# Output projections of two branches as streams of their own beside attention, and weights loaded once per layer

## Chip, cores and metric

The kernel runs on one core of a Trainium2 chip. The metric is the device time of one execution in microseconds (us), the median of several runs.

## What is computed

One inference step of a backbone with two layers, over 1024 latent and 128 context tokens (T = 1152, nine blocks of 128), model width 1024. Cut to what the change touches:

```python
h = RMSNorm(x) * (1 + scale) + shift
P = h @ W_in                       # columns for three mixers A, B, C, their paths z, and merge logits G
o_A = diff_attention(...)          # 4 heads, two softmax maps each
o_B = retention, both directions   # 4 heads
o_C = gated DeltaNet, both directions   # 4 heads
y_b = (norm(o_b) * silu(z_b)) @ W_b              # W_b: 512 x 1024, for each of the three branches
x = x + gate * ((sum_b sigmoid(G_b) * y_b) @ W_out)   # W_out: 1024 x 1024
```

Branch 0 is A, 1 is B, 2 is C.

## The kernel before

Activations lie feature by token: `hH` and `hL` hold the 1024 features of all 1152 tokens as a high and a low part. A product of full precision is made from three matmuls, high x high, high x low and low x high. A weight block is therefore loaded (512 KB, DMA queue of SyncE), cast to its high part on ScalarE (L362) and subtracted to its low part on GpSimd (L363), all in `load_w`. Two shapes use it: `proj_feat` (L403: 24 matmuls of 384 tokens for a third of one block of 128 features) and `proj_tok` (L382: 24 matmuls of 256 features for 128 tokens). Working memory is 25 large buffers of 1160 values a partition (`pg`), 8 of 512 (`pm`) and a region of small ones (`lo`).

Each layer is a set of streams, written as generators: `rp0`, `rp1` (projections of retention heads 0, 1 and 2, 3, `ret_proj`), `rm0`, `rm1` (their chunks, `ret_mix`), `fk`, `fq`, `fv`, `mid`, `pp`, `scan` for each DeltaNet head, `av`, `prep`, `mix` for attention (`att_v`, `att_prep`, `att_mix`), twelve `z` and 24 `g` streams for paths and merge gates, `ada` for the modulation and `fin` for the final stage. The class `Emitter` issues one piece of a stream at a time. A chain stream (`CHAIN`) goes first when its latency has passed on an estimated clock, otherwise the first in the table `BULK` that may run; a stream starts when the streams that it names are done and `NEED` large buffers are free. What is issued is then ordered once more on each engine by the framework's scheduler, with leads given to some (`LEAD`, `EVAC`). Projections so stand between the steps of the chains on TensorE.

`scan` runs over the four DeltaNet heads, and `mix` behind it over the four attention heads. One step of `mix` is a block of 128 queries: two transposes of the query (L1447), 12 score matmuls against the keys (L1467), maxima on VectorE (L1468), exponentials on ScalarE (L1471), the weighted difference of the two maps on VectorE (L1478, once per step), nine transposes of it (L1489) and the products with the values (L1498). `rp1` waits for the last `prep` and `rm1` for the last `mix`.

Each head's output goes through `put_o` into DRAM (`osc`), each merge gate's tanh into `ssc`. The final stage (`finish`) takes three blocks of 384 tokens one after the other. For a block and each branch, in the order C, A, B, it loads the outputs and splits them (L1545, L1546), then goes through four weight blocks of `w_branch`: a unit is 12 matmuls of 384 columns (L1598), a gate load (L1592), and VectorE's product with the gate (L1601, L1603) and sum (L1604); the last branch's sums go into `hH` and `hL` (L1606, L1607). Then eight weight blocks of `w_out` are multiplied, 256 features at a time (L1637), gated and added to x (L1643, L1644), and normed for the next layer (`norm_rows`, `norm_cols`: L619, L632, L639). So all weights of the stage are loaded and split three times per layer: 36 blocks of `w_branch` and 24 of `w_out`.

Of the kernel before, what the change touches and what calls it, by code (L numbers as in the profile page):

```python
# [13 lines left out]
DEPTH = 2  # L14
NT = 9
NL = 8
# [25 lines left out]
BULK = "rp0 z20 g22 fk1 fk0 z10 fq2 g23 z11 fq1 g20 g21 fq0 fv0 g24 g00 fk3 fv1 gate0 g26 g25 g05 fv2 z21 fk2 g27 z22 prep0 z00 g03 z23 g01 fv3 g02 prep1 av0 fq3 g07 g04 g11 z13 z02 rp1 prep2 z03 g10 g06 z01 g14 g15 g12 g17 prep3 z12 av1 ada g16 g13 fin".split()  # L42
NEED = {'rp': 10, 'rm': 6, 'fk': 6, 'mid': 4, 'fq': 5, 'fv': 6, 'pp': 2, 'scan': 1, 'av': 10, 'prep': 9, 'mix': 5, 'z': 3, 'g': 3, 'gate': 5, 'ada': 6, 'fin': 10}
# [228 lines left out]
class Build:  # L272
# [3 lines left out]
    def run(self, upto=None):  # L276
        nc, tc = self.nc, self.tc
        with ExitStack() as ctx:
# [25 lines left out]
            self.zsc = [[[dr([128, T], f"zsc{i}_{b}_{h}") for h in range(NH)] for b in range(3)] for i in L]  # L304
            self.m1 = [[dr([72, 1024], f"m1_{i}_{h}") for h in range(NH)] for i in L]
# [129 lines left out]
    def layer(self, l):  # L435
# [17 lines left out]
        add("rm0", self.ret_mix(l, 0, r[0]), ("rp0",))  # L453

# [14 lines left out]
        add("rp1", self.ret_proj(l, 1, r[1]), ("prep3",))  # L469
        add("rm1", self.ret_mix(l, 1, r[1]), ("rp1", "mix3"))  # L470

# [10 lines left out]
        rest = [n(x) for x in gs + zs + ["rp1"] + ["ada"] * (not last)]  # L482
        add("fin", self.finish(l, rest), ["scan3", "mix3", "rp1", "g26", "g27"] + ["gate0"] * (l == 0))
# [301 lines left out]
    def ret_proj(self, l, p, s):  # L785
        nc, ar = self.nc, self.ar
        if p == 0:
            cs = self.load_cs()
# [17 lines left out]
        (cs if p == 0 else self.att["cs"]).free()  # L806
# [553 lines left out]
    def att_prep(self, l, h):  # L1360
# [63 lines left out]
        if h == NH - 1:  # L1424
            self.att["wq"].free()

# [104 lines left out]
    def finish(self, l, rest):  # L1531
        nc, ar, ap = self.nc, self.ar, self.ap
        last = l == DEPTH - 1
        gate = None
        orr = Ring(ar, 384, 3)
        BR = (2, 0, 1)

        def load_o(tb, br):
            blocks = [ar.alloc(PAGE, True) for _ in range(3)]
            hl = []  # L1540
            for h in range(NH):
                o = orr.next().v(384)
                nc.sync.dma_start(out=o, in_=self.osc[l][br][h][:, tb * 384:tb * 384 + 384])
                x = [blocks[i // 3].ap[:, (i % 3) * 384:(i % 3) * 384 + 384] for i in (2 * h, 2 * h + 1)]
                nc.scalar.copy(x[0], o)  # L1545
                nc.vector.tensor_tensor(out=x[1], in0=o, in1=x[0].bitcast(F32), op=ALU.subtract)  # L1546
                hl.append(x)
            return blocks, hl

        todo = [(tb, br) for tb in range(3) for br in BR]  # L1550
        names = {1: "rm1", 2: "scan3", 0: "mix3"}
        pend = []

        def ahead():
            if todo:
                tb, br = todo[0]
                if tb == 0:
                    yield (f"{names[br]}.{l}", f"g{br}6.{l}", f"g{br}7.{l}")
                    self.store(0)
                todo.pop(0)  # L1560
                pend.append(load_o(tb, br))

        seq = []
        for _ in range(3):
            seq += [ap["w_branch"][l, br, :, fp * 256:fp * 256 + 256] for br in BR for fp in range(4)]
            seq += [ap["w_out"][l, q * 512:(q + 1) * 512, n * 256:(n + 1) * 256] for n in range(4) for q in range(2)]
        held = []

        def weights():
# [3 lines left out]
            return held.pop(0)  # L1573

        yield from ahead()
        for tb in range(3):
            c = slice(tb * 384, tb * 384 + 384)
            acc = [ar.alloc(T) for _ in range(3)]
            yv = [acc[f // 3].v(3, 384)[:, f % 3] for f in range(8)]
# [130 lines left out]
```

## Time and profile before

| | |
|---|---|
| median of 3 runs | 3506.38 us (3504.82 to 3514.66) |
| profiled execution | 3519.01 us, span 3517.2 us, mean granted TensorE clock 0.955 |
| TensorE matmul / weight load busy | 92% / 88% |
| VectorE, ScalarE, GpSimd busy | 62%, 41%, 33% |
| DMA | 340 MB, mean 97 GB/s |

In the profile PE is TensorE's matmul, PEld its weight load, DVE VectorE, ACT ScalarE, POOL GpSimd and SP SyncE. Matmuls are pipelined, and the duration of one, some 0.3 us, is longer than the distance between the starts of two; so the price of a matmul is read from a dense run, its length over its count, and not from its mean. A line can be a helper's: L362 and L363 stand for all weight splits. The granted clock is 1.00 at 2.4 GHz and 0.50 at 1.2 GHz.

### The profile page before, as it was taken

The page shows a single profiled execution, that of the slowest core. Times are in us where ns is not written, and L with a number is a line of the kernel's source. Part 1 is how long each engine was busy: PE and PEld are TensorE (multiplying, and loading weights), DVE is VectorE, ACT ScalarE, POOL GpSimd, SP SyncE. Part 2 cuts the span into 40 slices and gives each one's busy share as a digit, 9 for nine tenths or more (in the row PEclk, how much of TensorE's full clock was granted, in tenths as well). Part 3 has the DMA queues.
Part 4 walks back from the last instruction along what each step waited for, and adds up shares of the span by engine and source line. Part 5 has one row for each costly group of instructions (what it writes and reads, how often), then busy time and mean ns, then how long its engine had stood idle before and what let it go on. Part 6 is the DMA issues. An engine that isn't in the chain of part 4 may idle for free. (4 is left out here: it accounts for less than half of the span.)

```text
span 3517.2 us, 61428 instructions
## 1 busy us (share of the span) xinstructions
PE 3231.1 (92%) x23275; PEld 3086.3 (88%) x23275; DVE 2171.8 (62%) x5053; ACT 1439.6 (41%) x4110; POOL 1144.2 (33%) x1134
## 2 busy tenths in 40 slices
PE   6999999999999987778899999999999998787899
PEld 5998899998998887668899998999999997786898
DVE  6555646645735775667675556665457376666776
ACT  4334444533434444433333354443434344443232
POOL 3122433244310430144551224332453133102454
PEclk7999999999999998889999999999999998899999
DMA  6134223232144011356541323222221210013665
GB/s 209 44 115 125 75 81 88 83 84 68 37 139 135 24 32 38 98 168 201 186 140 51 110 71 96 85 74 82 81 71 38 81 35 29 26 32 124 224 215 173
DMA packets 353723, 340.07 MB, mean 97 GB/s; under 512 B 57108, under 2 KB 325778, under 8 KB 353426
## 3 DMA queue, kind: packets, MB, share of 16 engines
q1 hardware_dynamic: 353426, 336.14, 30.4%
q8 instruction: 183, 3.00, 0.3%
q14 instruction: 114, 0.93, 0.1%
HBM read 262.50 MB, written 73.56 MB: 96 GB/s over the span
## 5 line engine op out<-in xcount | busy, mean ns | idle before, releaser
L403 PE MATMUL ps<-hH,pg 128*128 128x384 f32 x4608 | 1249.7, 345 | 11.8 <-ACT pg L667 4.7
L363 POOL TENSOR_TENSOR pg<-pg,pg 128x1024 fp32r<-128x1024 f32 x256 | 630.6, 2470 | 1117.0 <-ACT pg L362 675.8
L403 PEld LDWEIGHTS ps<-hH,pg 128*128 128x128 f32 x4608 | 838.7, 190 | 19.4 <-ACT pg L667 6.3
L403 PE MATMUL ps<-hL,pg 128*128 128x384 f32 x2304 | 792.3, 344 | 0.0
L382 PE MATMUL ps<-pg,hH 128*128 128x256 f32 (+1 forms) x2880 | 565.0, 291 | 22.1 <-POOL pg L363 5.4
L382 PEld LDWEIGHTS ps<-pg,hH 128*128 128x128 f32 x2880 | 462.0, 193 | 28.9 <-POOL pg L363 6.6
L403 PEld LDWEIGHTS ps<-hL,pg 128*128 128x128 f32 x2304 | 437.0, 190 | 1.2
L362 ACT CAST pg<-pg 128x1024 fp32r<-128x1024 f32 (+1 forms) x256 | 267.6, 1048 | 395.3 <-DMA pg<-in_w_in 144.9
L382 PE MATMUL ps<-pg,hL 128*128 128x256 f32 (+1 forms) x1440 | 414.1, 288 | 0.0
L1598 PE MATMUL ps<-pg,pg 128*128 128x384 f32 x1728 | 331.0, 352 | 44.0 <-ACT pg L362 19.2
L1598 PEld LDWEIGHTS ps<-pg,pg 128*128 128x128 f32 x1728 | 317.1, 198 | 51.9 <-ACT pg L362 21.5
L382 PEld LDWEIGHTS ps<-pg,hL 128*128 128x128 f32 x1440 | 277.5, 193 | 0.1
L341 POOL TENSOR_TENSOR lo<-lo,kc 128x3 f32<-128x3 f32 (+4 forms) x88 | 132.3, 1505 | 441.6 <-DVE lo L1524 125.4
L1467 PE MATMUL ps<-pg,pm 128*128 128x384 f32 x768 | 210.8, 377 | 43.3 <-ACT pg L1471 43.1
L1468 DVE TENSOR_REDUCE lo<-ps 128x1 f32<-128x384 f32 (+1 forms) x350 | 182.5, 540 | 100.4 <-PE ps L1467 97.5
L1471 ACT ACTIVATE pg<-ps,lo 128x384 f32<-128x384 f32 (+1 forms) x350 | 196.1, 570 | 101.5 <-DVE lo L1469 100.0
L1637 PE MATMUL ps<-pg,hH 128*128 128x256 f32 x1152 | 216.9, 291 | 11.9 <-ACT hH L1606 10.8
L1637 PEld LDWEIGHTS ps<-pg,hH 128*128 128x128 f32 x1152 | 186.4, 199 | 14.3 <-ACT hH L1606 13.0
L1467 PEld LDWEIGHTS ps<-pg,pm 128*128 128x128 f32 x768 | 133.9, 203 | 60.1 <-ACT pg L1471 55.6
L1637 PE MATMUL ps<-pg,hL 128*128 128x256 f32 x576 | 167.6, 292 | 7.3 <-DVE hL L1607 6.7
L1498 PE MATMUL ps<-pg,pg 128*128 128x128 f32 x1072 | 153.0, 292 | 4.3 <-ACT pg L1494 2.5
L1498 PEld LDWEIGHTS ps<-pg,pg 128*128 128x128 f32 x1072 | 145.9, 207 | 8.4 <-ACT pg L1494 4.7
(315 smaller groups left out, 5328.3 us busy)
## 6 DMA issues: line engine op xcount, KB each, us to landing
pg<-in_w_in SPq DMA_DIRECT2D x112, 512.0 KB
pg<-in_w_branch SPq DMA_DIRECT2D x72, 512.0 KB
ssc<-pg SPq DMA_DIRECT2D x144, 192.0 KB
pg<-ssc SPq DMA_DIRECT2D x144, 192.0 KB
pg<-in_w_ada SPq DMA_DIRECT2D x48, 512.0 KB
pg<-in_w_out SPq DMA_DIRECT2D x48, 512.0 KB
pg<-gsc SPq DMA_DIRECT2D x32, 576.0 KB
zsc<-pg SPq DMA_DIRECT2D x72, 192.0 KB
```

Source lines behind the costliest of these rows:

```text
L341: self.nc.gpsimd.tensor_tensor(out=out, in0=in_, in1=self.mh[0:in_.shape[0], 0:in_.shape[1]], op=ALU.pow)
L362: nc.scalar.copy(h, r)
L363: (nc.vector if dve else nc.gpsimd).tensor_tensor(out=lo, in0=r, in1=h.bitcast(F32), op=ALU.subtract)
L382: nc.tensor.matmul(out=out, lhsT=a[:, k, t * 128:t * 128 + 128], rhs=x[:, k % 4, :], start=i == 0, stop=i == 23)
L403: nc.tensor.matmul(out=out, lhsT=w[:, k, :], rhs=a[:, k, tb * 384:tb * 384 + 384], start=i == 0, stop=i == 23)
L1467: nc.tensor.matmul(out=self.ps[:, b, 0:w], lhsT=q[:, i, m], rhs=k, start=i == 0, stop=i == 1)
L1468: nc.vector.tensor_reduce(out=s[:, m * 3 + c:m * 3 + c + 1], in_=self.ps[:, b, 0:w], op=ALU.max, axis=AX.X)
L1471: nc.scalar.activation(out=p.v(T)[:, c * w:c * w + w], in_=self.ps[:, bs[c], 0:w], func=AF.Exp, bias=s[:, 6 + m:7 + m], accum_out=s[:, 8 + ...
L1498: nc.tensor.matmul(out=oo, lhsT=x[:, i * 128:i * 128 + 128], rhs=v, start=kt == 0, stop=kt == nkt - 1)
L1598: nc.tensor.matmul(out=out, lhsT=ww[:, h, fi * 128:fi * 128 + 128], rhs=a, start=i == 0, stop=i == 11)
L1637: nc.tensor.matmul(out=out, lhsT=a, rhs=ww[:, f, :], start=j == 0, stop=j == 23)
```

## The change

- The retention heads 2 and 3 (`rp1`, `rm1`) follow heads 0 and 1 at the layer's start and no longer wait for attention. The tables of the rotary angles are kept for them.
- A new stream `branch(l, br, bi)` makes one branch's output for all 1152 tokens: it loads and splits the four heads' outputs whole (4 x 2 large buffers), loads four weight blocks once, and goes through 24 units (8 features blocks x 3 token blocks) of 12 matmuls. `br1` (branch B, after `rm1` and its gates) writes its gated outputs into a new DRAM array `ysc`; `br2` (branch C, after `br1` and `scan3`) loads them, adds, and stores the sums there again. Both are bulk streams that need 14 free large buffers, late in `BULK`.
- `finish` starts after `br2` and the last `mix`. It runs branch A, which loads the sums from `ysc` and writes `hH` and `hL`, then loads all of `w_out` once, as eight blocks of 256 x 512, and multiplies with 512 columns at a time. Token blocks 0 to 5 are done with both halves of the features; the last three with one half after the other, so that the norm of earlier blocks stands between products.
- `BULK` is another order of all streams; `NEED` has new entries.

```diff
-BULK = "rp0 z20 g22 fk1 fk0 z10 ... prep3 z12 av1 ada g16 g13 fin".split()
+BULK = "z11 rp1 rp0 fk0 z10 fq0 ... prep3 prep2 z02 g04 br1 br2 g06 g05 z03 ada g02 g01 g07 fin".split()
-... 'ada': 6, 'fin': 10}
+... 'ada': 6, 'fin': 16, 'br': 14}
...
+        add("rp1", self.ret_proj(l, 1, r[1]), ("rp0",))
+        add("rm1", self.ret_mix(l, 1, r[1]), ("rp1", "rm0"))
...
-        add("rp1", self.ret_proj(l, 1, r[1]), ("prep3",))
-        add("rm1", self.ret_mix(l, 1, r[1]), ("rp1", "mix3"))
...
-        add("fin", self.finish(l, rest), ["scan3", "mix3", "rp1", "g26", "g27"] + ["gate0"] * (l == 0))
+        add("br1", self.branch(l, 1, 0), ["rm1"] + [f"g1{f}" for f in range(8)])
+        add("br2", self.branch(l, 2, 1), ["br1", "scan3"] + [f"g2{f}" for f in range(8)])
+        add("fin", self.finish(l), ["br2", "mix3"] + gs + zs + ["gate0"] * (l == 0) + ["ada"] * (not last))
...
+    def branch(self, l, br, bi):
...
+        last = bi == 2
+        seq = [ap["w_branch"][l, br, :, fp * 256:fp * 256 + 256] for fp in range(4)]
...
+        for h in range(NH):
+            o, hb, lb = ar.alloc(T), ar.alloc(T, True), ar.alloc(T, True)
+            nc.sync.dma_start(out=o.v(T), in_=self.osc[l][br][h])
+            nc.scalar.copy(hb.v(T), o.v(T))
+            nc.vector.tensor_tensor(out=lb.v(T), in0=o.v(T), in1=hb.v(T).bitcast(F32), op=ALU.subtract)
...
+        tr = Ring(ar, 384, 3)
+        pr = Ring(ar, 384, 3) if bi else None
+        for fp in range(4):
+            w, wh, wl = weights()
+            for fi in range(2):
+                f = 2 * fp + fi
+                for tb in range(3):
+                    c = slice(tb * 384, tb * 384 + 384)
+                    t = tr.next().v(384)
+                    nc.sync.dma_start(out=t, in_=self.ssc[l][br][f][:, c])
+                    y = t
+                    if bi:
+                        y = pr.next().v(384)
+                        nc.sync.dma_start(out=y, in_=self.ysc[l][f][:, c])
+                    out = self.ps[:, self.bank(1, (0, 1, 2, 3)) if last else self.bulk(), 0:384]
...
+                            nc.tensor.matmul(out=out, lhsT=ww[:, h, fi * 128:fi * 128 + 128], rhs=a.v(T)[:, c], start=i == 0, stop=i == 11)
...
+                        nc.vector.scalar_tensor_tensor(out=t, in0=t, scalar=1.0, in1=out, op0=ALU.add, op1=ALU.mult)
+                    if bi:
+                        nc.vector.tensor_tensor(out=y, in0=y, in1=t, op=ALU.add)
+                    if last:
+                        nc.scalar.copy(self.hH[:, f, c], y)
+                        nc.vector.tensor_tensor(out=self.hL[:, f, c], in0=y, in1=self.hH[:, f, c].bitcast(F32), op=ALU.subtract)
+                    else:
+                        self.late.append((self.ysc[l][f][:, c], y))
+                        self.store(1)
...
+    def finish(self, l):
...
+        yield from self.branch(l, 0, 2)
+        ws = {}
+        for n in range(2):
+            for q in range(4):
+                ws[n, q] = self.load_w([ap["w_out"][l, q * 256:(q + 1) * 256, n * 512:n * 512 + 512]], 2)
...
+        for t in range(6):
+            for n in range(2):
+                product(t, n)
+                yield 5.5, 0, 1.4
+            if t % 3 == 2 and not last:
+                self.norm_rows(block(t // 3))
+            if t == 3:
+                cols(0)
+        for n in range(2):
+            for t in range(6, 9):
+                product(t, n)
...
```

How TensorE's order moves, at head 3 of attention in layer 0. Before, a stretch in the middle of that head (L1467 scores, L1489 transposes, L1498 values, L1447 query):

```order
L1498 MATMUL ps<-pm_9_1210,pg_766_11618 128x128
L1467 MATMUL ps<-pg_776_11959,pm_125_11620 128x384 x2
L1489 MATMUL ps<-kc,pg_803_12648 128x128 x6
L1467 MATMUL ps<-pg_776_11959,pm_125_11620 128x384 x2
L1489 MATMUL ps<-kc,pg_803_12648 128x128 x2
L1467 MATMUL ps<-pg_776_11959,pm_125_11620 128x384 x2
L1498 MATMUL ps<-pg_671_10265,pg_766_11618 128x128 x4
L1489 MATMUL ps<-kc,pg_803_12648 128x128
L1498 MATMUL ps<-pg_671_10265,pg_766_11618 128x128 x4
L1447 MATMUL ps<-kc,pm_124_11619 128x128 x2
```

Now, a stretch of the same head (L1470 scores, L1501 values, L1492 transposes, L1450 query, L1577 branch B's matmuls):

```order
L1470 MATMUL ps<-pg_815_12997,pm_146_13262 128x384 x2
L1577 MATMUL ps<-pg_845_13303,pg_854_13348 128x384
L1577 MATMUL ps<-pg_789_12302,pg_854_13348 128x384
L1577 MATMUL ps<-pg_845_13303,pg_855_13349 128x384
L1470 MATMUL ps<-pg_815_12997,pm_146_13262 128x384 x2
L1577 MATMUL ps<-pg_803_12370,pg_854_13348 128x384
L1577 MATMUL ps<-pg_770_11718,pg_854_13348 128x384
L1577 MATMUL ps<-pg_803_12370,pg_855_13349 128x384
L1470 MATMUL ps<-pg_815_12997,pm_146_13262 128x384 x2
L1577 MATMUL ps<-pg_837_13293,pg_854_13348 128x384
L1501 MATMUL ps<-pg_537_7925,pg_805_12375 128x128 x8
```

Before, the nine query blocks of that head have nothing else between them; now branch matmuls stand between the score matmuls of one query block and between its parts.

How SyncE's order of transfers moves. Before, in the final stage (L1592 a gate load, L360 a weight load):

```order
L1592 DMA pg_2209_30088<-ssc_0_2_124 128x384
L360 DMA pg_2122_29598<-in_w_branch 128x4x256
L1592 DMA pg_2209_30088<-ssc_0_3_125 128x384
L360 DMA pg_2191_29995<-in_w_branch 128x4x256
L1592 DMA pg_2209_30088<-ssc_0_4_126 128x384
L360 DMA pg_2255_30307<-in_w_branch 128x4x256
L1592 DMA pg_2209_30088<-ssc_0_5_127 128x384
```

Now, in branch C (L680 a store of a sum into `ysc`, L1571 the load of an earlier sum, L1567 a gate load):

```order
L680 DMA ysc_0_170<-pg_900_14172 128x384
L1567 DMA pg_899_14171<-ssc_2_1_115 128x384
L680 DMA ysc_0_170<-pg_900_14172 128x384
L1571 DMA pg_900_14172<-ysc_1_171 128x384
L1567 DMA pg_899_14171<-ssc_2_1_115 128x384
L1571 DMA pg_900_14172<-ysc_1_171 128x384
```

Where a gate load alternated with a weight load, each unit now has a store, a load of a sum into a slot that a store has left, and a gate load.

## Rows read from the trace of the kernel before

**Rows 1.** Busy time of the engines, from the page.
```profile
PE 3231.1 (92%) x23275; PEld 3086.3 (88%) x23275; DVE 2171.8 (62%) x5053; ACT 1439.6 (41%) x4110; POOL 1144.2 (33%) x1134
```

**Rows 2.** Stretches: us, then PE, PEld, DVE, ACT, POOL busy, clock, DMA, GB/s.
```profile
1334.00:1435.00 101.00, 75.33 (x464) 66.43 (x463) 61.95 (x164) 48.23 (x166) 1.80 (x1) 0.86 0.11 34
1435.00:1560.00 125.00, 96.25 (x512) 86.43 (x513) 78.75 (x172) 39.89 (x106) 37.03 (x16) 0.86 0.44 139
1560.00:1810.00 250.00, 223.51 (x1489) 218.77 (x1489) 177.97 (x248) 90.42 (x132) 124.09 (x56) 0.93 0.59 192
2955.00:3044.00 89.00, 62.92 (x362) 56.42 (x363) 65.33 (x176) 46.73 (x157) 16.73 (x25) 0.83 0.03 8
3087.00:3124.00 37.00, 37.00 (x302) 36.91 (x301) 22.05 (x56) 17.15 (x61) 0.00 (x0) 1.00 0.06 18
3124.00:3166.00 42.00, 30.95 (x174) 27.57 (x172) 25.49 (x71) 19.60 (x69) 0.00 (x0) 0.84 0.05 15
3166.00:3290.00 124.00, 94.60 (x542) 85.61 (x541) 82.94 (x175) 41.77 (x111) 39.57 (x16) 0.90 0.49 161
3290.00:3517.00 227.00, 210.74 (x1415) 205.91 (x1413) 155.38 (x197) 65.82 (x86) 115.30 (x46) 0.96 0.59 197
1640.00:1665.00 25.00, 25.00 (x145) 25.00 (x144) 24.13 (x28) 8.50 (x13) 15.30 (x6) 1.00 0.77 246
```

**Rows 3.** Line L1478 in four stretches, in order: filled, bare, bare, bare.
```profile
L1478 DVE SCALAR_TENSOR_TENSOR pg<-pg,lo,pg x4: 1408/1416/1420, 3087.5 to 3123.7; 128x1152 f32<-128x1152 f32 x4
L1478 DVE SCALAR_TENSOR_TENSOR pg<-pg,lo,pg x9: 351/1417/1419, 1360.6 to 1434.6; 128x1152 f32<-128x1152 f32 x8, 128x128 f32<-128x128 f32 x1
L1478 DVE SCALAR_TENSOR_TENSOR pg<-pg,lo,pg x9: 341/1407/1420, 2954.8 to 3043.1; 128x1152 f32<-128x1152 f32 x8, 128x128 f32<-128x128 f32 x1
L1478 DVE SCALAR_TENSOR_TENSOR pg<-pg,lo,pg x5: 1407/1419/1420, 3111.8 to 3157.7; 128x1152 f32<-128x1152 f32 x5
```

**Rows 4.** Six steps of bare attention: lines L1467, L1489, L1498, in this order.
```profile
1368.80:1425.40 56.60, 21.82 (x72) 13.01 (x72) 0.87 0.00 1
1368.80:1425.40 56.60, 11.67 (x54) 9.37 (x54) 0.87 0.00 1
1368.80:1425.40 56.60, 15.65 (x108) 15.51 (x108) 0.87 0.00 1
```

**Rows 5.** The chain that ended last: start, us, what, 3290 to 3517.
```profile
3290.62 2.42 DMA pg<-ssc
...
3299.35 26.71 PE ps L1637 x224
...
3326.06 4.23 PE ps L1598 x24
...
3331.36 4.98 DMA pg<-osc
...
3349.25 16.19 PE ps L1598 x91
...
3376.32 6.57 DMA pg<-ssc
...
3390.11 30.63 PE ps L1637 x241
```

**Rows 6.** Groups by line: count, busy us, mean ns, idle before.
```profile
L363 POOL TENSOR_TENSOR pg<-pg,pg 128x1024 fp32r<-128x1024 f32 x256 | 630.6, 2470 | 1117.0 <-ACT pg L362 675.8 <-PE ps L403 77.2 <-PE ps L1489 62.2
...
L362 ACT CAST pg<-pg 128x1024 fp32r<-128x1024 f32 (+1 forms) x256 | 267.6, 1048 | 395.3 <-DMA pg<-in_w_in 144.9 <-DMA pg<-in_w_branch 91.1 <-DMA pg<-in_w_out 53.8
...
L1604 DVE TENSOR_TENSOR pg<-pg,pg 128x384 f32<-128x384 f32 x96 | 100.0, 1044 | 1.7
...
L905 PE MATMUL ps<-pg,pm 128*128 128x128 f32 x144 | 29.4, 291 | 5.7 <-ACT pm L910 5.4
```

**Rows 7.** Line L1604: ns least, median, most; first and last start.
```profile
L1604 DVE TENSOR_TENSOR pg<-pg,pg x96: 541/557/2744, 1484.2 to 3478.5; 128x384 f32<-128x384 f32 x96
```

**Rows 8.** What TensorE waited for: us, times, longest.
```profile
PE ps L1598 <- DVE pg L639: 14.1, 2, 8.5
```

More of the change, by code (lines that the diff above doesn't have):

```diff
@@ L304, in run @@
             self.zsc = [[[dr([128, T], f"zsc{i}_{b}_{h}") for h in range(NH)] for b in range(3)] for i in L]
+            self.ysc = [[dr([128, T], f"ysc{i}_{f}") for f in range(8)] for i in L]
             self.m1 = [[dr([72, 1024], f"m1_{i}_{h}") for h in range(NH)] for i in L]
@@ L787, in ret_proj @@
         if p == 0:
-            cs = self.load_cs()
+            self.rcs = self.load_cs()
         qk = s["qk"] = [ar.alloc(T) for _ in range(2)]
@@ L805, in ret_proj @@
         ring.free()
-        (cs if p == 0 else self.att["cs"]).free()
+        if p == 1:
+            self.rcs.free()
         vv = s["vv"] = [ar.alloc(T) for _ in range(2)]
@@ L1425, in att_prep @@
             self.att["wq"].free()
+            self.att["cs"].free()
     def att_mix(self, l, h):
@@ L1528, in att_mix @@
         st2.free()
-    def finish(self, l, rest):
+    def branch(self, l, br, bi):
         nc, ar, ap = self.nc, self.ar, self.ap
[L1533 to L1566, printed above, removed]
+        last = bi == 2
+        self.store(0)
+        seq = [ap["w_branch"][l, br, :, fp * 256:fp * 256 + 256] for fp in range(4)]
         held = []
@@ L1609, in finish @@
-                    yield 3.9, 0
-                for x in blocks:
-                    x.free()
-            tr.free()
-            for x in acc:
-                x.free()
-            yield from ahead()
-            if gate is None:
-                gt = Ring(ar, 256, 2)
-                gate = [ar.alloc(1024) for _ in range(2)]
-                for i in range(2):
-                    nc.sync.dma_start(out=gate[i].v(1024), in_=self.md[l][i:i + 1].to_broadcast([128, 1024]))
-            xt = []
@@ L1646, in finish @@
-            for i in range(3):
-                nc.sync.dma_start(out=self.x_out(l, tb * 3 + i), in_=xt[i].v(1024))
-            if not last:
-                self.norm_rows(xt)
-                self.norm_cols(l + 1, tb, xt)
-            for x in xt:
-                x.free()
-        for x in (gt, orr, self.sg, self.lamb, *gate, self.vec[l], self.scol[l]):
+                    if last:
[4 more added lines that the diff above has]
+                        self.store(1)
@@ new lines, in branch @@
+                    if fp == 3 and fi == 1 and tb == 2:
+                        self.free_w(w)
+                        for x in hl:
+                            self.free_w(x)
+                        if last:
+                            tr.own[0].free()
+                            pr.own[0].free()
+                    elif fi == 1 and tb == 2:
+                        self.free_w(w)
+                    yield 2.1, 0, 1.1 if bi else 0.6
+        if not last:
+            self.store(0)
+            tr.free()
+            pr and pr.free()
```

118 lines of the change are left out of this document (59 added, 59 removed).

## Prediction

> **What bounds the kernel now.** I read the profile's page first: TensorE is busy for 92% of the span, VectorE is the next at 62% [rows 1]. So TensorE's work is the floor, and a gain must come from stretches in which it waits or runs at the lower of its two levels (1.2 of 2.4 GHz). Second, a table of stretches [rows 2]. TensorE is full at clock 1.00 in 3087 to 3124, while attention's steps have other matmuls between them, and loses time in two kinds of places, in both layers: attention steps with nothing between them (1334 to 1435, 2955 to 3044, 3124 to 3166: about 70% busy, clock 0.83 to 0.86), and all that follows attention (1435 to 1810, 3166 to 3517: second half of the retention, then the final stage). Third, attention's own pace, by one VectorE instruction per step (L1478) [rows 3]. Three filled steps span 36.2 us (12.1 each); eight bare ones 74.0 in layer 0 (9.25 each); in layer 1 eight bare ones 88.3 (11.0) and four more 45.9 (11.5). Fourth, the chain that ended last, in the last 230 us [rows 5]: dense runs of L1637, and between them L1598 in pieces, broken by transfers of 2.4 to 6.6 us.
>
> **What those stretches lose.** Prices at full clock come from dense runs: 16.19 us for 91 matmuls of 384 columns is 0.178, 26.71 for 224 of 256 is 0.119 [rows 5]; a matmul of 128 columns I put at 0.126 (108 in 15.65 us at clock 0.87 [rows 4]; 0.145 x 0.87).
> - A bare step has 12 score matmuls, 9 transposes and 18 value matmuls (72, 54 and 108 in six steps [rows 4]) and two query transposes: 12 x 0.178 + 29 x 0.126 = 5.8 us. Loss: 8 x (9.25 - 5.8) = 28 in layer 0; 8 x (11.0 - 5.8) + 4 x (11.5 - 5.8) = 65 in layer 1. Together 93, or 4.6 per step.
> - Behind attention, each layer must do 864 matmuls of 384 and 864 of 256: 153.8 + 102.8 = 256.6. The retention half has some 174 of 128 columns (L905 has 144 for four such halves, 36 each [rows 6]; its sister lines make the rest): 22. Nine output transposes for three heads, 3.4, and in layer 0 72 of the norm, 9. So layer 0 needs 291 and takes 375 (loss 84), layer 1 needs 282 and takes 351 (loss 69).
> All of it: 246 us.
>
> **What the change removes, adds and moves.**
> Moved: the second retention half now starts behind the first, in a stretch full of projections, and its 22 us of TensorE work fills gaps or adds to a busy engine as before; its loss, inside the 84 and 69, goes. It brings VectorE work to the first 250 us of each layer, hidden under projections; without that cover it would cost what it cost in 1435 to 1560, some 30 us a layer. The outputs of branches 1 and 2 (576 matmuls a layer, 102 us) move from behind attention into it. By the order of TensorE, head 3 of the attention, bare before in layer 0, has branch matmuls between its steps; but the stream waits until 14 of the 25 large buffers are free, so bare steps remain in head 2: I count six in layer 0 and five in layer 1. At 4.6 each, 51 us stay. Bounds: 3.45 (layer 0's) to 5.7 (layer 1's), so 38 to 63.
> Behind attention stay 480 branch matmuls in layer 0 and 459 in layer 1: 40 and 38 units of 12. A unit is 2.14 us at full rate. In the final stage of before, 24 units take 3326.06 to 3390.11, 2.67 each [rows 5], and this I take: 78 x 0.53 = 41 us of loss. Reasons for 2.67 here: the new units move more. A unit of the last branch loads the gate and the sum (2 x 192 KB), and 12 weight loads of 512 KB fall into its 24 units: 15.7 MB in 51 us would be 305 GB/s, where 25 us of before had 246 GB/s at a DMA share of 0.77 [rows 2], so full use is about 320. Bounds: 2.14 (no loss) and 3.3 (two transfers one after the other at 3.7 us, midway between 2.42 and 4.98, two VectorE instructions of 0.55 and two issues, 9.1 us, over three ring slots is 3.05; a bit more for the queue): 0 to 90 us.
> Start of the last branch: its input needs the last head's output stored, loaded and split. From the last output transposes to the first matmul of that branch stand 121 and 108 matmuls of branch 2, 21 and 19 us; a load of such an input took 4.98 [rows 5], so a store, a load and a split of under 3 us each fit. I cost it at nothing; without that cover, 10 us a layer.
> The product with w_out: 864 matmuls of 512 columns for 1728 of 256. The trace has no 512. Both widths that it has cost 0.464 ns per column (0.119/256, 0.178/384), so I take 0.237, against twice 0.119: 1 us gained. Bounds: 5% either way, 10 us gained or lost. Norm, last weights and tail I put at 5 us a layer, 10: before, the norm alone made TensorE wait 14.1 us [rows 8], now products of other blocks stand between; the last three weight loads go into buffers that the last branch frees, 5 us and a split late at worst (0 to 24 for both layers).
> Removed: 80 of the 256 weight splits (2470 ns on GpSimd and 1048 on ScalarE [rows 6]: 198 and 84 us), and 42 MB of loads. Added: 192 transfers of 192 KB, 38 MB, half of them stores. GpSimd and ScalarE are under 42% busy, so I cost both at nothing except through the units' pace. The order of the projections changes throughout; I take the other stretches as unchanged, give or take 20.
> Sum: 51 + 41 + 10 = 102 remain of 246: 144, and 1 for the width, 145. The profiled execution took 3519.0 (span 3517.2), 12.6 over the median of 3506.4, so 3506 - 145 = about **3360 us**.
>
> One rule bears on the pace of a unit. The row: L1604, a VectorE add of two SBUF operands, took 541 ns at least, 557 in the median and 2744 at most [rows 7], 1044 in the mean [rows 6]. The Trainium skill (SBUF — State Buffer, SBUF: two separate sides) says that VectorE with two SBUF inputs and a GpSimd instruction lock each other out for a whole instruction. The maximum, which is a median plus most of a 2470 ns split, agrees. By that rule fewer splits mean quicker units, which is the second rival.
>
> **Rivals.**
> 1. The sums' round trip sets the pace of branch 2 after attention: SP is in order, a load of a sum into a ring slot waits until the store from that slot has landed, and behind it wait the next gate and weight loads, then VectorE, then one of two PSUM banks. For: loads of 6.57 us on the chain [rows 5]. Against: three slots. If the 30 units of branch 2 behind attention take 4.6 (9.1 us over two slots) and the last branch's 48 take 3.0: 58 + 16 more, 3434.
> 2. Units run clean, since splits on GpSimd no longer hold VectorE (557 ns against 2744 [rows 7]): 80 fewer, and the branch under attention meets few. Units at 2.2 give 37 back, bare steps at 3.45 give 13: 3310. Against: the last branch still has 12 splits in 24 units, as dense as before.
> 3. Slower: the three ring slots, parts of one buffer, do not overlap at all, so each of the 96 units that go through DRAM pays the whole round trip, 6.6 us with the shortest load (2.42 [rows 5]) twice. Per layer 48 units then take 317 us where head 3 (110) and the 40 reckoned behind it hide 150: 3360 + 2 x 167 = 3694. It decides from 4.6 us per unit on: there 48 units eat the 73 us that a layer gains. Against: the gate loads of before run from the same kind of ring at one per 2.7 us.
> 4. No gain: with the retention in front and another order of projections, the earlier stretches lose 70 us a layer more. In rows 2 nothing points to it; every projection stays available as filler.
>
> **How the numbers follow.** Forecast 0.50, rival 1 0.16, rival 2 0.25, rival 3 0.05, rival 4 0.04 (half of it slower). What a measurement can tell from no change is 0.3%, 10.5 us. Faster 0.50 + 0.16 + 0.25 and a little of rival 4: 0.91; same 0.02; slower 0.07. Range: from 3285 (units clean, bare steps at the low bound, and 20 us from the other stretches) to 3430 (rival 1).
>
> **What would show it.** Right: no retention between attention and the final stage; a last stretch of some 200 us per layer (85 of branches and 102 of w_out, plus their losses) instead of 375 and 351; attention's steps at about 12 us in head 3 with TensorE full; eleven bare steps at 9 to 11 us; 176 weight splits on GpSimd. Wrong: VectorE waiting on loads of the sums for more than 40 us in all (rival 1, or 3 when branch units come at over 4.6 us); L1604's successor at a mean near 560 ns and units at 2.2 (rival 2); more TensorE waits before the first attention step than before (rival 4).

## The result, and the profile after

The changed kernel took 3423.19 us in the median of four runs (3421.57 to 3424.89), the kernel before 3509.87 (3504.82 to 3514.66): a ratio of 0.9753, 95% interval 0.9736 to 0.9771. Forecast were 3360 and a range of 3285 to 3430. The direction holds and the time lies in the range, but 87 us were gained where 145 were forecast. Of the difference of 58, 7 come from the profiled executions: before's lay 9 us above its median, the changed kernel's 2. The other 51 are in the trace: spans of 3517.2 and 3423.1 us, 94 apart.

To find them I divide the span as the prediction did. The loss of a stretch is its length less its matmuls at the prediction's prices (0.178, 0.126, 0.119 us, and 0.237 for 512 columns). The 3400 matmuls of other shapes, the same number in both kernels, are counted with some 213 us. The matmuls' own price then hardly differs between the kernels, 3167 and 3166 us, so the whole gain is lost time that went, 350.5 to 257.2:

| loss, both layers, us | before | forecast | after |
|---|---|---|---|
| bare steps of attention (before: 12 of it in two steps beside a `prep`) | 93 | 51 | 46.7 |
| steps beside the last `prep` (before: layer 0 alone) | 19.6 | 19.6 | 45.8 |
| the step in which head 2 becomes head 3 | 0 | 0 | 27.9 |
| filled steps of head 3 (the prices are a little high) | 0 | 0 | -4.5 |
| from the step in which branch 2 begins to the layer's end (before: from the end of attention) | 153 | 51 | 68.7 |
| all the rest | 84.9 | 84.9 | 72.6 |
| sum | 350.5 | 206.5 | 257.2 |

The 93 and the 153 of before are the prediction's own sums, and the last row is what is left. Counted as after, the bare steps of before lost about 90 (32 in 1360.6 to 1434.6, 39 in 2954.8 to 3043.1, 19 in 3123.7 to 3166.9), and the end of its change of heads in layer 0 some 7 (1347.0 to 1360.6).

The engines of the changed kernel, from the page, beside [rows 1]; the span is shorter and every engine does less:

```profile
PE 3177.8 (93%) x22411; PEld 3017.1 (88%) x22411; DVE 2021.2 (59%) x4933; ACT 1350.7 (39%) x3982; POOL 940.3 (27%) x1054
```

The stretches of the table, layer 0 and then layer 1, with the columns of [rows 2]: steps beside the last `prep`, bare steps, the change of heads, filled steps of head 3, branch 2 beginning, branch 2's rest with the last branch, and w_out (layer 1 without filled steps):

```profile
1264.00:1343.00 79.00, 55.69 (x369) 51.41 (x369) 64.17 (x198) 34.50 (x111) 35.83 (x52) 0.85 0.18 57
1343.00:1401.00 58.00, 44.61 (x246) 39.17 (x246) 40.76 (x95) 34.41 (x111) 0.00 (x0) 0.82 0.04 11
1401.00:1423.00 22.00, 13.49 (x57) 11.34 (x58) 12.07 (x22) 7.17 (x21) 6.43 (x3) 0.65 0.32 102
1423.00:1500.00 77.00, 77.00 (x489) 76.21 (x489) 48.18 (x110) 32.52 (x105) 4.84 (x3) 0.99 0.44 143
1500.00:1557.00 57.00, 49.53 (x292) 47.87 (x291) 38.99 (x75) 20.46 (x48) 11.45 (x5) 0.94 0.71 226
1557.00:1653.00 96.00, 78.62 (x414) 76.35 (x413) 59.22 (x93) 21.06 (x31) 20.09 (x8) 0.93 0.76 247
1653.00:1758.00 105.00, 105.00 (x480) 85.66 (x479) 52.30 (x95) 29.88 (x53) 19.59 (x15) 1.00 0.33 112
2978.00:3006.00 28.00, 18.00 (x105) 15.69 (x104) 25.20 (x84) 14.22 (x46) 14.34 (x24) 0.82 0.26 85
3006.00:3064.00 58.00, 43.25 (x246) 37.84 (x246) 41.70 (x99) 35.34 (x115) 0.00 (x0) 0.85 0.04 11
3064.00:3085.00 21.00, 13.78 (x58) 11.45 (x58) 11.80 (x22) 6.70 (x19) 6.58 (x3) 0.64 0.33 107
3162.00:3220.00 58.00, 51.08 (x301) 49.59 (x300) 39.72 (x70) 19.29 (x47) 11.38 (x5) 0.94 0.70 223
3220.00:3316.00 96.00, 78.50 (x403) 76.26 (x402) 58.40 (x89) 21.16 (x31) 19.75 (x8) 0.91 0.75 241
3316.00:3418.00 102.00, 100.85 (x434) 81.06 (x432) 31.32 (x47) 6.06 (x8) 9.78 (x4) 1.00 0.27 99
```

Read the clock column first: 0.99 and 1.00 where steps are filled and in w_out, 0.65 and 0.64 in the change of heads. VectorE is 81 and 90% busy in the two stretches beside the last `prep` (64.17 of 79, 25.20 of 28).

The weighted difference, once a step as in [rows 3], in the filled steps and in the bare ones of each layer:

```profile
L1481 DVE SCALAR_TENSOR_TENSOR pg<-pg,lo,pg x5: 1406/1411/1420, 1433.9 to 1487.1; 128x1152 f32<-128x1152 f32 x5
...
L1481 DVE SCALAR_TENSOR_TENSOR pg<-pg,lo,pg x6: 1408/1414/1419, 1342.9 to 1392.8; 128x1152 f32<-128x1152 f32 x6
...
L1481 DVE SCALAR_TENSOR_TENSOR pg<-pg,lo,pg x6: 1406/1414/1419, 3006.3 to 3055.3; 128x1152 f32<-128x1152 f32 x6
```

A filled step takes 13.3 us (53.2 over four), TensorE full; a bare one 10.0 and 9.8, of which 5.8 is work.

The change of heads, in the order of time (start, duration, engine, line, and in brackets the idle time before it and what ended it). SP's row is the issue of the weight loads, two of them:

```profile
1408.15 6.06 SPq L361 DMA_DIRECT2D pg<-in_w_branch  x2
1409.98 1.15 ACT L1553 CAST pg<-pg 128x1152 fp32r<-128x1152 f32 x1 [0.91 <-DMA pg<-osc]
1412.60 1.54 PE L714 MATMUL ps<-kc,pg 128*128 128x128 f32 x6 [4.25 <-DVE pg L708]
1419.60 1.04 ACT L363 CAST pg<-pg 128x1024 fp32r<-128x1024 f32 x1 [0.99 <-DMA osc<-pg]
1420.69 1.65 PE L1577 MATMUL ps<-pg,pg 128*128 128x384 f32 x4 [1.19 <-ACT pg L363]
```

Head 2's last values end, VectorE and GpSimd finish its scaling, the output is transposed, head 3's first query is prepared, and only then does branch 1's first matmul come. The chain has nothing beside it. That matmul waits for the cast of its weights for 1.19 us only, and the cast's bracket names a store of head 2's output, not the weight load, as what it waited for last. TensorE is idle for 8.5 of these 22 us, half of it just before the output's transposes. So the branch stands behind these waits in TensorE's order; and had it stood ahead of them, its weights, cast at 1419.60, would not have been there.

The start of the last branch in layer 0: three rows of TensorE's timeline, then the cast and the issue that it waited for:

```profile
1575.24 12.60 PE L1577 MATMUL ps<-pg,pg 128*128 128x384 f32 x60 [3.61 <-DVE pg L1580]
1594.99 39.95 PE L1577 MATMUL ps<-pg,pg 128*128 128x384 f32 x216 [7.16 <-ACT pg L363]
1638.74 14.38 PE L1577 MATMUL ps<-pg,pg 128*128 128x384 f32 x72 [3.79 <-ACT hH L1584]
```

```profile
1574.90 1.15 ACT L1553 CAST pg<-pg 128x1152 fp32r<-128x1152 f32 x1 [1.92 <-DMA pg<-osc]
1593.90 1.04 ACT L363 CAST pg<-pg 128x1024 fp32r<-128x1024 f32 x1 [17.85 <-DMA pg<-in_w_branch]
```

```profile
1586.95 2.05 SPq L361 DMA_DIRECT2D pg<-in_w_branch  x2
```

The last head's input is cast at 1574.9; the first weights are issued at 1586.95, behind branch 2's sums on SP's queue, and cast at 1593.9. Once running, 18 of its 24 units take 39.95 us, 2.22 each; the next comes after another wait of 3.79 us.

Groups by line, beside [rows 6]: weight splits on GpSimd, and the sum's add with its wait for the load.

```profile
L364 POOL TENSOR_TENSOR pg<-pg,pg 128x1024 fp32r<-128x1024 f32 (+1 forms) x176 | 431.2, 2454 | 1173.7 <-ACT pg L363 689.4 <-DVE pg L1554 197.3 <-PE ps L577 68.4
...
L1582 DVE TENSOR_TENSOR pg<-pg,pg 128x384 f32<-128x384 f32 x96 | 64.4, 672 | 46.9 <-DMA pg<-ysc 46.3
```

And the longest piece of the chain that ended last, which prices a matmul of 512 columns at 94.99 / 408 = 0.233:

```profile
3322.84 94.99 PE ps L1634 x408
```

### The profile page after: what moved, and what is told of

It reads as the page before. It is cut to its first block, busy times and chain, and to the rows that moved or that the text cites. A ratio compares the mean times of both kernels' runs of the same rounds, so it can differ in the third digit from the quotient of the medians.

```text
span 3423.1 us, 59260 instructions
## 1 busy us (share of the span) xinstructions
PE 3177.8 (93%) x22411; PEld 3017.1 (88%) x22411; DVE 2021.2 (59%) x4933; ACT 1350.7 (39%) x3982; POOL 940.3 (27%) x1054
## 5 line engine op out<-in xcount | busy, mean ns | idle before, releaser
L404 PE MATMUL ps<-hH,pg 128*128 128x384 f32 x4608 | 1266.6, 346 | 14.4 <-DVE pg L689 4.3
L364 POOL TENSOR_TENSOR pg<-pg,pg 128x1024 fp32r<-128x1024 f32 (+1 forms) x176 | 431.2, 2454 | 1173.7 <-ACT pg L363 689.4
L383 PE MATMUL ps<-pg,hH 128*128 128x256 f32 (+1 forms) x2880 | 557.2, 289 | 18.0 <-POOL pg L364 5.8
L383 PEld LDWEIGHTS ps<-pg,hH 128*128 128x128 f32 x2880 | 457.2, 191 | 23.0 <-POOL pg L364 6.4
L1577 PE MATMUL ps<-pg,pg 128*128 128x384 f32 x1728 | 341.8, 352 | 46.6 <-ACT pg L363 20.1
L1577 PEld LDWEIGHTS ps<-pg,pg 128*128 128x128 f32 x1728 | 315.1, 197 | 53.9 <-DVE pg L1580 23.6
L363 ACT CAST pg<-pg 128x1024 fp32r<-128x1024 f32 (+1 forms) x176 | 184.2, 1049 | 254.2 <-DMA pg<-in_w_in 114.6
L1032 DVE SCALAR_TENSOR_TENSOR pg<-pg,lo,pg 128x384 f32<-128x384 f32 (+2 forms) x288 | 206.8, 725 | 71.3 <-ACT pg L1030 66.9
L1470 PE MATMUL ps<-pg,pm 128*128 128x384 f32 x768 | 213.3, 378 | 34.3 <-ACT pg L1474 34.0
L342 POOL TENSOR_TENSOR lo<-lo,kc 128x12 f32<-128x12 f32 (+3 forms) x91 | 137.2, 1510 | 374.2 <-DVE lo L1391 117.7
L1470 PEld LDWEIGHTS ps<-pg,pm 128*128 128x128 f32 x768 | 137.4, 204 | 51.3 <-ACT pg L1474 47.0
L1634 PE MATMUL ps<-pg,hH 128*128 128x512 f32 x576 | 180.8, 395 | 1.0 <-ACT pg L363 1.0
L1501 PE MATMUL ps<-pg,pg 128*128 128x128 f32 x1040 | 147.6, 293 | 6.5 <-DVE pg L1495 4.7
L1501 PEld LDWEIGHTS ps<-pg,pg 128*128 128x128 f32 x1040 | 141.2, 208 | 10.7 <-DVE pg L1495 5.5
L779 POOL TENSOR_TENSOR pg<-pg,pg 128x128 f32<-128x128 f32 x192 | 97.3, 521 | 133.8 <-ACT pg L795 94.6
```

Of the source, the lines that this page charges most:

```text
L342: self.nc.gpsimd.tensor_tensor(out=out, in0=in_, in1=self.mh[0:in_.shape[0], 0:in_.shape[1]], op=ALU.pow)
L363: nc.scalar.copy(h, r)
L364: (nc.vector if dve else nc.gpsimd).tensor_tensor(out=lo, in0=r, in1=h.bitcast(F32), op=ALU.subtract)
L383: nc.tensor.matmul(out=out, lhsT=a[:, k, t * 128:t * 128 + 128], rhs=x[:, k % 4, :], start=i == 0, stop=i == 23)
L404: nc.tensor.matmul(out=out, lhsT=w[:, k, :], rhs=a[:, k, tb * 384:tb * 384 + 384], start=i == 0, stop=i == 23)
L1032: nc.vector.scalar_tensor_tensor(out=o, in0=x[:, lo + s:hi + s], scalar=wcol(s), in1=o, op0=ALU.mult, op1=ALU.add)
```

## Experiments

My first theory (A) was that the missing time lies in attention before branch 1's first matmul, and that filling these steps gives it back; the rival (B) that it lies behind attention. Each ratio is against the kernel before on the same chip. TensorE's order is the same until well behind the first score in all of these kernels, and yet the first score came at 1018.8 to 1027.3 us in their profiled executions: the sum of a single trace says nothing below 8 us.

**The two parts of the change apart.** e1_behind lets branches 1 and 2 wait for attention:

```diff
-        add("br1", self.branch(l, 1, 0), ["rm1"] + [f"g1{f}" for f in range(8)])
+        add("br1", self.branch(l, 1, 0), ["rm1", "mix3"] + [f"g1{f}" for f in range(8)])
```

> The changed kernel with one dependency more: branch 1's stream also waits for the last attention head (mix3), so branches 1 and 2 run behind attention and nothing runs beside head 3. Theory A (a filled step is worth what a bare one loses): head 3's nine steps of each layer become bare, 18 x 4.1 us (mean loss of the twelve quiet bare steps at 1343 to 1401 and 3006 to 3064) = 74; about 14 more units a layer of branch 2 run behind attention at some 3.1 us against 2.2, 25; one more late start of a branch a layer, 7 each. 3423 + 74 + 25 + 14 = 3536, no faster than the kernel before. Rival (what is filled beside attention is given back by attention's own pace, so that the gain comes from the rest of the change): within 30 us of 3423.

Measured: 3549.59, ratio 1.0081 (1.0053 to 1.0108). As theory A says: 126 us slower than the changed kernel. Loss from the first score to the last rises from 58.9 to 90.9 in layer 0 and from 74.7 to 104.2 in layer 1, and behind it from 48.5 to 104.4 in both: 61 us in attention, where 74 were expected, and 56 behind it, where 39 were.

e2_ret is the kernel before with the retention's second half in front:

```diff
+        add("rp1", self.ret_proj(l, 1, r[1]), ("rp0",))
+        add("rm1", self.ret_mix(l, 1, r[1]), ("rp1", "rm0"))
...
-        add("rp1", self.ret_proj(l, 1, r[1]), ("prep3",))
-        add("rm1", self.ret_mix(l, 1, r[1]), ("rp1", "mix3"))
```

> The kernel before with one part of the change alone: the second retention half starts behind the first, and the list of priorities is that of the changed kernel without br1 and br2; the final stage is that of before (all three branches, blocks of 384 columns, weights loaded three times). By the prediction's own sum the retention's part of the loss behind attention goes, some 25 to 40 us a layer, so 3430 to 3460. Theory A (loss is set by how many attention steps have nothing beside them): the projections that stood between the steps of head 3 in before now stand elsewhere, all of heads 2 and 3 is bare, 127 as in the changed kernel plus 18 x 4.1 = 74, the final stage loses some 90 as before and the rest 110: 401 us of loss against 397 in before, so 3500 to 3530, no gain.

Measured: 3526.36, ratio 1.0024 (1.0007 to 1.004). The prediction's own sum fails here and theory A holds. Behind attention 52.6 us of loss go and before it 22, but attention's loss rises by 87 (32.3 to 85.5 and 69.7 to 103.4): with this list of priorities the projections that stood between its steps are done earlier. The move and the list were not tried apart. Neither e1_behind nor e2_ret gains anything.

**Starting branch 1 earlier.** e3_early:

```diff
+... 'br': 14, 'br1': 11}
...
-        tr = Ring(ar, 384, 3)
+        tr = Ring(ar, 384, 3) if bi else self.sg
...
-            while seq and len(held) < (FD if held else 1):
+            while seq and len(held) < (FD if held and (bi or self.room() >= 5) else 1):
```

> The changed kernel, with branch 1 able to start in 11 free large buffers instead of 14: its gate rows use the ring that the projections' streams have left, and its next weights are loaded ahead only while five large buffers are free. By the order of TensorE some 160 branch matmuls a layer move from behind attention into the second half of head 2 and the change of heads. Theory A (the missing 60 us lie in the bare stretch before branch 1's first matmul, 73 us in layer 0 and 53 in layer 1): 160 x 0.178 = 28 us a layer go, 3423 - 56 = about 3365 (3345 to 3385), with the first branch matmul some 40 us earlier against the first score. Rival B (they lie behind attention, in the sums' round trip and the late start of the last branch): within 12 us of 3423.

Measured: 3418.86, ratio 0.9708 (0.9682 to 0.9733): no gain that can be told apart, so theory A fails as I had put it. Some 180 branch matmuls a layer now run before the last score, and attention is longer by as much; its loss is 132.7 instead of 133.6. TensorE's waits from 1320 to 1570 show why; L1580 is the branch's matmul, L717 the transposes of a head's output:

```profile
PE ps L1580 <- ACT pg L363: 9.0, 3, 5.6
PE ps L717 <- DVE pg L711: 4.3, 1, 4.3
```

That the waits on weights come from the loads that are no longer ahead is argued here; e5_half tries it.

e5_half makes room for loads ahead:

```diff
-        seq = [ap["w_branch"][l, br, :, fp * 256:fp * 256 + 256] for fp in range(4)]
+        seq = [ap["w_branch"][l, br, :, f * 128:f * 128 + 128] for f in range(8)]
...
+        rb, wb = hi.alloc(512, False), hi.alloc(1024, True)
+        r, h, lo = rb.v(512), wb.ap[:, 0:512], wb.ap[:, 512:1024]
```

> The changed kernel with the weights of a branch loaded and split in pieces of 128 columns (256 KB, high and low part in one large buffer) instead of 256, one or two pieces ahead, and gate rows in the projections' ring: a branch needs 11 or 12 large buffers with its loads ahead, and branch 2 no longer waits between the branches. By the order some 268 branch matmuls a layer (48 us) move from behind attention into heads 2 and 3. The earlier start without loads ahead moved 180 and gained nothing: attention grew by 32 us a layer, with waits of 9.0 and 6.7 us on weights and of 10.7 and 12.1 us of loss left in the step at the change of heads. Theory A1 (that gain was lost to the missing loads ahead and to the gap between the branches): bare steps and the change of heads lose 30 to 35 us a layer less, 3350 to 3365. Rival A2 (what bounds these steps is the chain of one step through ScalarE, VectorE and TensorE, which a matmul in between lengthens by its own time): attention grows by about the 48 us, 3410 to 3425.

Measured: 3398.27, ratio 0.9658 (0.9632 to 0.9684), 25 us better than the changed kernel: between A1 and A2. The change of heads and the step behind it, in both layers, with the columns of [rows 2]:

```profile
1420.00:1455.00 35.00, 33.86 (x210) 33.17 (x209) 15.88 (x34) 7.26 (x21) 5.77 (x4) 1.00 0.63 188
1455.00:1476.00 21.00, 11.18 (x48) 10.26 (x47) 9.83 (x20) 9.52 (x23) 3.52 (x3) 0.76 0.79 252
...
3072.00:3106.00 34.00, 34.00 (x213) 33.68 (x212) 17.36 (x35) 7.05 (x20) 5.63 (x4) 1.00 0.66 197
3106.00:3125.00 19.00, 12.04 (x44) 10.84 (x43) 9.95 (x19) 9.74 (x23) 4.10 (x3) 0.71 0.86 275
```

The change of heads is full at clock 1.00: a stream that runs already does cover it. But 27 us of filler (34.7 of work less the 7.6 of the step itself) go where 14 were lost, branch 1 is used up, and branch 2's first loads open a new gap of 13.2 and 11.8 us of loss right behind it. So attention's loss falls by 10 us only (133.6 to 123.8 over both layers); as much of the gain lies behind attention (48.5 to 37.4).

e6_halfpre loads each branch's first piece in the branch before:

```diff
+            if f == 7 and not last:
+                self.pre = self.load_f(ap["w_branch"][l, (2, 0)[bi], :, 0:128])
```

> As the kernel with half pieces, and each branch's first piece is loaded by the branch before it. The same edit by itself gained some 14 us. If the late first weights at the last branch's start and the loss in attention are separate terms: 10 to 16 us below the kernel with half pieces. If smaller pieces have already made the start quick: the same as that within 5 us.

Measured: 3411.14, ratio 0.9688 (0.9659 to 0.9718): not better. With branch 2 used up beside attention, the last branch waits for its input instead of its weights (L1566 casts the last head's output):

```profile
1603.01 12.43 PE L1591 MATMUL ps<-pg,pg 128*128 128x384 f32 x60 [12.22 <-ACT pg L1566]
```

That is about the 10 us a layer that the prediction named for a lost cover. But e5_half has as few branch matmuls left behind the last score (36 of branch 2's 288) and waits 3.1, 2.0 and 2.1 us at this place; why it is more here is not shown.

e10_halfring gives e5_half six slots for the sums:

```diff
+            pr = Ring(ar, 384, 3)
+            p2 = Ring(ar, 384, 3)
+            pr.b, pr.own = pr.b + p2.b, pr.own + p2.own
```

> The kernel with half pieces and an early start, with six ring slots for the sums besides. There branch 2 runs almost wholly beside head 3, and SP waited 16.5 us between 1455 and 1480 for stores of sums, with weight loads behind it. Theory R2 (the sums' ring holds SP up, and with it the weights): the waits of branch matmuls on weight casts (11.8 and 8.6 us) shrink to less than half, 5 to 15 us faster than with three slots, 3383 to 3393. Rival (branch 2's first matmul waits for its split input in TensorE's order whatever the ring): within 5 us of 3398.

Measured: 3413.68, ratio 0.9704 (0.9684 to 0.9724). Theory R2 falls: TensorE's wait for weight casts in layer 0 stays.

```profile
PE ps L1593 <- ACT pg L684: 12.3, 2, 7.1
```

Why it is some 15 us slower than e5_half is open. 7 of the 8 us between their traces lie before the first score, where their instructions are the same; but the longer ring also makes branch 2 wait for 13 free large buffers instead of 12, 504 branch matmuls a layer stand before the last score instead of 540, and attention loses 134 us instead of 124. So the slots were not tried alone here.

**The last `prep`.** e11_norope leaves the rotary step of head 3's preparation out:

```diff
-                if u < NL:
+                if u < NL and h < NH - 1:
```

> The changed kernel without the rotary step of the last attention head's preparation (its 8 blocks of 128 rows stay unrotated): some 19 us of VectorE less per layer, in the steps that run beside that preparation (43 of L782 and 25 of L783 between 1264 and 1343). Theory V (these six steps a layer-pair lose 47 us because VectorE, 82 to 99% busy there, holds the weighted differences back): their loss falls towards the 4.1 of a quiet bare step, 12 to 24 us less over both layers, 3400 to 3411. Rival (they lose what a bare step loses by its own chain, and the preparation only makes the step longer): within 6 us of 3423.

Measured: 3411.9, ratio 0.9692 (0.9667 to 0.9717), against 3420.99 of the changed kernel beside it: 9 us, under the expected 12, and the intervals overlap. In the trace the loss of these stretches falls from 32.0 to 25.6 and from 13.8 to 5.4. The median does not show it, but the traces speak for the rotary step's work as a cause, and not for all of it. The edit takes that step's products on GpSimd away with VectorE's, so VectorE is not shown to be the one.

**Behind attention.** e4_w0 loads each branch's first weights in the branch before (`NEED` falls with it, to 14 for `fin` and 12 for `br2`):

```diff
+            if fp == 3 and not last:
+                self.pre = self.load_w([ap["w_branch"][l, (2, 0)[bi], :, 0:256]], 4)
```

> The changed kernel, with each branch's first weights loaded by the branch before it, at that one's last fourth. Theory B1 (the last branch starts late because its first weight load stands at the end of SP's queue behind branch 2's sums: the cast at 1593.9 waited 17.8 us for it, while the last head's input was ready at 1577.8): the waits of 7.2 and 6.3 us at its start go, 2.2 and 2.3 at branch 2's start, and some us of the lower clock behind each: 18 to 26 us, about 3400. Rival (an earlier load only takes the queue from the sums): branch 2's last units grow as much, within 6 us of 3423.

Measured: 3409.46, ratio 0.9684 (0.966 to 0.9708). Theory B1 holds, with two thirds of its size: loss from the last score to w_out's end falls from 22.4 to 14.7 and from 26.1 to 18.6. (By the ratios alone the intervals of e4_w0 and of the changed kernel in e9_after just touch.)

e7_nosum leaves the sums out:

```diff
-                        nc.sync.dma_start(out=y, in_=self.ysc[l][f][:, c])
...
-                        nc.vector.tensor_tensor(out=y, in0=y, in1=t, op=ALU.add)
```

> The changed kernel without the sums: branches 2 and 0 neither load the sum of the branches before nor add it (192 KB and one VectorE add less for each of 96 units); stores stay, and the output holds branch 0 alone. Theory R (the sums' round trip sets the pace of branch 2's units behind attention: twelve units from 1547 to 1588 took 3.1 us or more each, VectorE waiting on these loads, while the last branch's first 18 took 2.2): the tail runs at 2.2, 9 to 14 us a layer less, about 3400; nothing changes beside head 3, where TensorE is full, nor in the last branch's pace. Rival (another cause, the gate rows' loads or two PSUM banks): within 6 us of 3423.

Measured: 3414.31, ratio 0.9704 (0.9676 to 0.9731): by the median less than theory R, and not clear of e9_after (0.9706 to 0.9753). The trace says more. From the last score to w_out's end:

```profile
1532.00:1763.00 231.00, 217.75 (x1108) 196.32 (x1107) 107.93 (x184) 58.19 (x101) 48.47 (x27) 0.97 0.47 150
3188.00:3408.00 220.00, 209.64 (x1050) 187.75 (x1048) 87.42 (x127) 33.55 (x54) 39.06 (x16) 0.98 0.45 147
```

The loss there falls from 48.5 to some 25 us, while attention's rises by 7 with fewer branch matmuls beside head 3 (301 before the last score, for 323 and 327). About half of the gain behind attention lies in the last branch, where none was expected: its units come at 2.2 us in the mean, for 2.4 and 2.5. Branch 2's tail stays slow, at 2.8 and 2.9 us a unit for 3.0. From 1532 to 1600 VectorE now waits for gate rows, and SP for the stores that must land before it may load into their slots:

```profile
DVE pg L1577 <- DMA pg<-ssc: 33.1, 16, 4.3
```

```profile
SPq L1567 <- DMA ysc<-pg: 33.9, 16, 5.9
```

So in branch 2's tail the load and the add are not what is slow: the slot is held until its store has landed, with the sum or without. (Without sums the store leaves from the gate row's slot, so the wait has moved to that ring.)

e8_ring6 has the six slots of e10_halfring in the changed kernel, and:

```diff
-        tr = Ring(ar, 384, 3)
+        tr = Ring(ar, 384, 3) if last else self.sg
```

> The changed kernel with six ring slots for the sums instead of three (gate rows move to the projections' ring, so the buffers needed are the same). Theory R: a load of a sum need no longer wait for the store from the same slot three units before; branch 2's tail goes from 3.1 us a unit towards 2.2, 5 to 10 us a layer less, 3405 to 3413. If SP's order or the gate rows set the pace: within 6 us of 3423.

Measured: 3415.09, ratio 0.9702 (0.9673 to 0.9732). By the median it cannot be told from the rival. In the trace the loss behind attention falls to 13.9 and 15.9, while attention's rises from 133.6 to 143.

e9_after is the changed kernel again, without an edit.

> The changed kernel once more, beside the others of this call, since the experiments so far differ from it by 8 to 25 us and shared a chip with the kernel before, not with it. All theories: a ratio to before of 0.973 to 0.977.

Measured: 3420.99, ratio 0.9729 (0.9706 to 0.9753), its loss split as in the first trace (59.0 and 75.7 in attention, 23.8 and 25.3 behind).

e12_both joins the edits of e4_w0 and e8_ring6.

> The changed kernel with two edits that were each tried alone: each branch's first weights loaded by the branch before it (3409, 12 to 14 us less than the changed kernel), and six ring slots for the sums (3415, 6 to 8 less). If they take away separate waits behind attention (the last branch's late first weights, the sums' slots): 3400 to 3405, and a loss behind attention of some 30 us over both layers against 50 in the changed kernel. If both only shorten the same wait in SP's queue, the weight loads behind the sums: 3407 to 3412.

Measured: **3390.94** (3380.47 to 3395.87), ratio 0.9643 (0.9627 to 0.9659): better than expected and the best of all versions, 30 us under the changed kernel. The loss behind attention is 3.1 and 4.5 us. The stretch from the last score to w_out's end, in the changed kernel:

```profile
1525.00:1758.00 233.00, 212.74 (x1073) 190.19 (x1072) 132.21 (x227) 58.53 (x102) 48.75 (x27) 0.97 0.56 183
3187.00:3418.00 231.00, 209.82 (x1025) 187.04 (x1023) 111.18 (x170) 34.09 (x55) 38.54 (x16) 0.96 0.53 177
```

and in e12_both:

```profile
1534.00:1742.00 208.00, 202.43 (x1040) 181.60 (x1040) 129.26 (x221) 59.16 (x102) 45.66 (x26) 0.99 0.59 197
3169.00:3373.00 204.00, 198.07 (x997) 177.38 (x995) 104.34 (x164) 34.53 (x55) 35.84 (x15) 0.99 0.58 194
```

TensorE is busy for 97% of it instead of 91. From the changed kernel's loss there, the first weights took away 15.2 us, the ring 18.7, both 40.9: separate waits, and a little more together. Two things go with it. This profiled execution took the least time of the four, 10 us under their median. And TensorE's order differs: 354 branch matmuls a layer stand before the last score (323 and 327 in the changed kernel), and 20 of w_out's stand among the last branch's (12 in e4_w0, 4 to 7 in e8_ring6, none in the changed kernel). What these moves give by themselves was not tried.

## Why the prediction was right and where it was wrong

- **Right: direction and mechanism.** What bounds the kernel is TensorE's lost time, and branch products beside head 3 fill it: filled steps run at clock 0.99 (13.3 us each, where about 12 were expected), and without that placement the change gains nothing (e1_behind, 1.0081). There are no retention matmuls between attention and the final stage, there are 176 splits, and from the last output transposes to w_out's end 201 us (1557 to 1758) and 197 (3221 to 3418), where some 200 were forecast.
- **The step that failed: "At 4.6 each, 51 us stay."** Its price and count were nearly right for bare steps alone (twelve, 46.7 us, 3.9 each). It left out two kinds of steps. Those beside the last `prep` have matmuls of it between them in the order, and so were not counted; but VectorE is 81 to 90% busy there, and they lose 45.8, 26 more than that row of before (14 more with the 12 us of before that the table has among the bare steps). And the step in which the heads change was taken as one of the filled ones, since the branch's first matmuls stand in it; but these come last in it, and it loses 27.9, at clock 0.65. With the 4 us that bare steps cost less, these are 50 of the 51. The other rows of the table nearly cancel (17.7 more, 4.5 and 12.3 less). e5_half shows that a stream already running covers that step, and by its trace e11_norope that the rotary step's work counts in the others. A reading of the prediction was off as well: the first of its "four more" bare steps, 3111.8 to 3123.7, is also the last of the three filled ones in [rows 3] and lost nothing. The 93 is some 6 us too high by that.
- **Mis-sized: what stays behind attention, 51 forecast, 68.7 measured.** "2.67 each, and this I take" had the wrong mechanism: 18 units of the last branch in layer 0 run at 2.22, close to the 2.2 of rival 2, and the others stand among waits. The mean behind the last output transposes came out near it, 2.85 (96 us for 34 units in layer 0 and for 33 in layer 1), but that is luck. The loss sits in branch 2's start and tail and in the last branch's start, which I cost at nothing: its input was in time, as worked out, but its first weights stood on SP's queue behind the sums. Two small edits remove 40.9 us of the 48.5 behind the last score in the trace (e12_both), 30 by the median.
- **The other stretches** gave back 12 us (84.9 to 72.6), inside the 20 allowed. They and the matmul of 512 columns (0.233 against 0.237) made no error.
- **The prediction took the terms as separate.** The retention's loss behind attention does go, but with the new priorities alone it comes back inside attention (e2_ret): the move pays only since branch products take the place of the projections that it uses up.
- **Rival 1** (the sums' round trip) showed its sign, 46.3 us of VectorE waiting for sums, but not its price: without any sums the kernel gains 7 to 9 us by the median, and some 24 behind attention in the trace, since a slot waits for its store all the same. **Rival 2**: the add's mean fell from 1044 to 672 ns with 176 splits for 256. The rule that it drew on (the Trainium skill, SBUF — State Buffer, SBUF: two separate sides) agrees with that direction, though no run tries the splits alone; its 3310 did not come, since the time was lost in waits and not in units. Rivals 3 and 4 did not happen.

What stays open: how much of the loss beside the last `prep` VectorE causes; why attention's loss rises when that behind it falls (e7_nosum, e8_ring6); and whether the earlier start of e5_half adds to e12_both, which was not tried.

## What to carry to other kernels

Count a stretch as covered only where the filler stands ahead of the waits in the engine's order and its operands are already there: the first matmul of a stream that has just begun may stand behind them, or wait for its own loads, and on an engine that takes its work in order everything behind it waits too (6.6 us at branch 2's first weights in e5_half). Filler is a fixed amount, so ask of each step what it will find beside it and what is then missing later; and look for loads of the next stage that stand on an in-order queue behind the stores of this one. A ring through DRAM holds a slot until its store has landed, so ask how many slots it needs, and not only what the added load and add cost: six slots took 19 us of loss away behind attention, leaving the sums out some 24, and the six slots with the earlier weights 41.

## What the runs showed of the hardware

In the change of heads a stall cost more than its wait: TensorE was idle for 8.5 of 22 us, the mean granted clock was 0.65, and the loss was 14.3 us; in e5_half, with branch matmuls in the step, the clock was 1.00. The same instruction order up to the first score took 1018.8 to 1027.3 us in thirteen profiled executions. A matmul of 512 float columns took 0.233 us, 0.455 ns a column, against 0.464 at 256 and 384.
